# State-space stage of a hybrid trunk layer: later sums and products, and a decay table made by ScalarE

## The chip, the cores and the metric

The kernel runs on one core of a Trainium2 chip. The metric is the device time of one execution in microseconds (us), lower is better. The engines are TensorE (PE in the rows; PEld is its weight load), VectorE (DVE), ScalarE (ACT), GpSimd (POOL) and SyncE (SP, which issues most transfers). Each engine works through its own queue in order; the engines wait for one another by semaphores.

## What is computed

One layer of a decoder trunk over 512 positions of width 1024, all in fp32. The part that matters here is the state-space branch, a complex diagonal recurrence over 32 groups of 16 channels with 64 states each:

```python
mag = jnp.exp(lam_re * dt)                 # decay of a state in one step
a_re, a_im = mag * jnp.cos(ang), mag * jnp.sin(ang)
bu = jnp.einsum('bsgp,gnp->bsgn', ug, bb)  # real and imaginary part
h[t] = a * h[t - 1] + bu[t]                # complex, by an associative scan
y = Re(einsum('gpn,bsgn->bsgp', c, h)) + d_skip * u
y = gelu(y);  y = y * sigmoid(y @ w_glu)
```

Beside it the layer has a short convolution, windowed attention, three gated merges, a SwiGLU block and a per-layer embedding.

## The kernel before

TensorE multiplies large weights all the time. Every fp32 weight is split in two halves of lower precision: ACT makes `hi` (L245), DVE makes `lo = raw - hi` (L246), and three matmuls (L287 to L289) make one product; their results are the tiles called `z`. The state-space stage lies inside this work. It is written as a generator, `ssm_gen` (L1003), one for each of four tiles of 128 channels (tile 0 to tile 3). The function `slot` advances all running generators by one step, between two stretches of 24 large matmuls; a new tile starts every four slots, so two or three tiles are in flight at a time.

Inside a stretch the function `pump` is called after every three matmuls. Two tables hang on it. `peq` is a queue: a function put there runs at one of the next pumps. `later(d, f)` puts `f` into the program at the d-th pump from now. So both decide only the place of an instruction in the program; on the chip each engine then takes its own instructions in that order.

The steps of one tile, with their lines:
- E = t4(0)·pre + t4(1)·pim (L1026 DVE, L1027 POOL into `ewt`, L1028 the sum on DVE, called E-sum below). W is made in the same way a slot later (L1067 to L1069), with the same buffer `ewt`.
- `e_all` (L1059): TensorE transposes E (L1039) and makes K products (L1047), the E products below; ACT copies ET (L1040), ko and dbuf (L1053, L1054), and SP sends parts of dbuf (L1057).
- `v_two` (L1077): the v products (L1083) of inputs and ET; then `rotate(0)` and, two pumps later, `rotate(1)`.
- `rotate` (L1088), for each half: DVE makes the decay table `mt` (L1092): the fourth power of the decay, one number for each partition and group of columns, with the first column of each 128 set to zero. ACT copies two halves into `vsw` (L1095, L1096), DVE multiplies G (L1098, which reads PSUM), POOL multiplies vsw (L1099). Three pumps later `rot_in`: G-sub on DVE (L1102), the scan R (L1104), ACT's copies gsw (L1107, L1108), the products sv (L1111) and, on POOL, gsw (L1112), and four pumps later their sum (L1114).
- Two slots on, ACT copies dbuf into Dg (L1123); the next slot's first pump runs the y products (L1130 with Dg, L1132 with sv and W). ACT copies ys (L1137), SP sends it through memory and back.
- Three slots on: yc (L1155 DVE), qq = yc² (L1157 POOL), `poly` (L1163, L1164 DVE), a sigmoid (L1167 ACT), yu (L1168 DVE) and its split yh (L283 ACT), yl (L284 DVE). This falls into the slot in which E of the tile two further on is made.

Of the kernel before, what the change touches and what calls it, by code (L numbers as in the profile page):

```python
# [9 lines left out]
F32 = mybir.dt.float32  # L10
F32R = mybir.dt.float32r
I32 = mybir.dt.int32
AF = mybir.ActivationFunctionType
ALU = mybir.AluOpType
# [27 lines left out]
C_CM = 640  # L42
# [35 lines left out]
def hybrid_trunk_kernel(  # L78
# [7 lines left out]
    pe, act, dve, pool, sp = nc.tensor, nc.scalar, nc.vector, nc.gpsimd, nc.sync  # L86
# [5 lines left out]
    def open_pool(stack, name, bufs=1, **kw):  # L92
        return stack.enter_context(tc.tile_pool(name=name, bufs=bufs, **kw))
# [16 lines left out]
    def ps_t():  # L110
        return pst.tile([128, 512], F32, tag="t", name="t")
# [7 lines left out]
    def ccol(i, n=1):  # L119
        return cst[:, i:i + n]  # L120
# [161 lines left out]
    def split_ap(src, hi, lo):  # L282
        act.copy(out=hi, in_=src)  # L283
        later(2, lambda: dve.tensor_tensor(lo, src, hi.bitcast(F32), ALU.subtract))  # L284
# [6 lines left out]
    peq = deque()  # L291
    fine = []

    def later(d, fn):
        if state["delay"]:
            due.setdefault(state["pump"] + d, []).append(fn)
        else:
            fn()
# [90 lines left out]
    mag4 = const.tile([128, 32], F32, tag="mag4", name="mag4")  # L389
# [560 lines left out]
    for pair in range(2):  # L950
        cc, acc = [], []
        for i in range(2):
            ps = z_tile()
            c = cvp.tile([128, T], F32, tag="cc", name="cc", bufs=2)
# [3 lines left out]
        for i in range(2):  # L958
# [5 lines left out]
            a = cvp.tile([128, T], F32, tag="acc", name="acc", bufs=2)  # L964
# [28 lines left out]
    sp_ = open_pool(sst, "ssm", 2)  # L993
# [6 lines left out]
    SC = [128, 4, 128]  # L1000


    def ssm_gen(ct):  # L1003
        rows = slice(ct * 128, (ct + 1) * 128)
        g0, c0 = ct * 8, ct * TBW
# [11 lines left out]
        def t4(i):  # L1017
            return t3(i).unsqueeze(2).to_broadcast(SE)

        def p4(tab, m0):  # L1020
            return tab[:, g0:g0 + 8, m0:m0 + 4].unsqueeze(3).to_broadcast(SE)

        yield
        E = sp_.tile(SE, F32, tag="EW", name="E", bufs=3)
        tmp = sp_.tile(SE, F32, tag="ewt", name="ewt", bufs=1)
        dve.tensor_tensor(E, t4(0), p4(pre, 1), ALU.mult)  # L1026
        pool.tensor_tensor(tmp, t4(1), p4(pim, 1), ALU.mult)  # L1027
        dve.tensor_tensor(E, E, tmp, ALU.add)  # L1028
        yield
        ET = sp_.tile(SC, F32, tag="ET", name="ET", bufs=1)  # L1030
        kps = []
# [27 lines left out]
        def e_all():  # L1059
# [1 line left out]
            k_two(0)  # L1061
            k_two(2)

        peq.append(e_all)
        W = sp_.tile(SE, F32, tag="EW", name="W", bufs=3)
        tmp = sp_.tile(SE, F32, tag="ewt", name="ewt", bufs=1)
        dve.tensor_tensor(W, t4(2), p4(pre, 0), ALU.mult)  # L1067
        pool.tensor_tensor(tmp, t4(3), p4(pim, 0), ALU.mult)
        dve.tensor_tensor(W, W, tmp, ALU.add)  # L1069
        cs = sp_.tile([128, 2, 8, 128], F32, tag="cs", name="cs", bufs=1)  # L1070
        sp.dma_start(out=cs.rearrange("p a g c -> p a (g c)"),
                     in_=tb_d[:, c0 + 512:c0 + TBW].rearrange("p (a n) -> p a n", a=2))
        yield
        vps, svs = {}, {}


        def v_two(a):  # L1077
            if a == 0:
                for b in range(2):
                    vps[b] = ps_t().rearrange("p (a c) -> p a c", a=4)  # L1080
            for b in range(2):
                r = slice(64 * b, 64 * b + 64)
                pe.matmul(vps[b][:, a], ET[r, a], uu[r, a], start=True, stop=True)  # L1083
            if a == 3:
                rotate(0)
                later(2, lambda: rotate(1))

        def rotate(h):  # L1088
            v3 = vps[h]
            cosT, sinT = cs[:, 0, h::2], cs[:, 1, h::2]  # L1090
            mt = sp_.tile(SC, F32, tag="mt", name="mt")
            dve.tensor_tensor(mt, mag4[:, g0 + h:g0 + 8:2].unsqueeze(2).to_broadcast(SC),  # L1092
                              ccol(C_CM, 128).unsqueeze(1).to_broadcast(SC), ALU.mult)
            vsw = sp_.tile(SC, F32, tag="sa", name="vsw")
            act.copy(out=vsw[0:64], in_=v3[64:128])  # L1095
            act.copy(out=vsw[64:128], in_=v3[0:64])  # L1096
            G = sp_.tile(SC, F32, tag="sb", name="G", bufs=3)
            dve.tensor_tensor(G, v3, cosT, ALU.mult)  # L1098
            pool.tensor_tensor(vsw, vsw, sinT, ALU.mult)  # L1099

            def rot_in():
                dve.tensor_tensor(G, G, vsw, ALU.subtract)  # L1102
                R = sp_.tile(SC, F32, tag="sa", name="R")
                dve.tensor_tensor_scan(R.rearrange("p g c -> p (g c)"), mt.rearrange("p g c -> p (g c)"),  # L1104
                                       G.rearrange("p g c -> p (g c)"), 0.0, ALU.mult, ALU.add)
                gsw = sp_.tile(SC, F32, tag="sc", name="gsw")
                act.copy(out=gsw[0:64], in_=R[64:128])  # L1107
                act.copy(out=gsw[64:128], in_=R[0:64])  # L1108
                sv = sp_.tile(SC, F32, tag="sb", name="sv", bufs=3)
                dve.memset(sv[:, :, 0:1], 0.0)  # L1110
                dve.tensor_tensor(sv[:, :, 1:128], R[:, :, 0:127], cosT[:, :, 0:127], ALU.mult)  # L1111
                pool.tensor_tensor(gsw, gsw, sinT, ALU.mult)  # L1112
                svs[h] = sv
                later(4, lambda: dve.tensor_tensor(sv[:, :, 1:128], sv[:, :, 1:128], gsw[:, :, 0:127], ALU.add))  # L1114

            later(3, rot_in)

        peq.append(lambda: [v_two(a) for a in range(4)])
        yield
        yield  # L1120
        for b in range(2):
            r = slice(64 * b, 64 * b + 64)
            act.copy(out=Dg[r, :, r].rearrange("p a (i q) -> p a i q", q=16),  # L1123
                     in_=dbuf[r].rearrange("p i a q -> p a i q"))
# [29 lines left out]
        yc = sp_.tile(SC, F32, tag="ya", name="yc", bufs=1)  # L1154
        dve.scalar_tensor_tensor(yc, un[:, ::-1, :], vecs[:, ct:ct + 1], yr, ALU.mult, ALU.add)  # L1155
        qq = sp_.tile(SC, F32, tag="un", name="qq", bufs=1)
        pool.tensor_tensor(qq, yc, yc, ALU.mult)  # L1157
        yu = sp_.tile([128, T], F32, tag="yb", name="yu", bufs=1)
# [5 lines left out]
            dve.tensor_tensor(qq, qq, yc, ALU.mult)  # L1164

        later(2, poly)
        later(4, lambda: act.activation(out=qq, in_=qq, func=AF.Sigmoid, scale=1.5957691216057308))  # L1167
        later(5, lambda: dve.tensor_tensor(yu.rearrange("p (c i) -> p i c", i=4)[:, ::-1, :], yc, qq, ALU.mult))  # L1168
        later(7, lambda: split_ap(yu, ybox[0][0][:, ct], ybox[0][1][:, ct]))
        yield  # L1170

# [3 lines left out]
    def slot():  # L1175
        if slot_n[0] in SSM_SLOTS:
            bg.append(ssm_gen(SSM_SLOTS[slot_n[0]]))
        slot_n[0] += 1
        step()
# [318 lines left out]
```

## Time and profile before

| what | us |
|---|---|
| median of three runs (856.53 to 858.35) | 856.62 |
| the profiled execution | 857.07 |
| its span in the trace | 855.3 |
| TensorE busy | 837.7 (98%) |
| DVE busy | 559.9 (65%) |
| ACT busy | 383.8 (45%) |
| POOL busy | 123.6 (14%) |

TensorE is the busiest engine by far, but the end of a matmul is modelled in the trace, so its busy share hides short gaps; the distance of two starts shows them. The state-space stage lies between about 176 and 320 us.

### The profile page before, as it was taken

The numbers are of one execution on the slowest core, as the hardware profiler recorded it, in microseconds if no ns is written. First come the engines' busy times: TensorE is split into PE (matmuls) and PEld (weight loads), VectorE is DVE, ScalarE is ACT, GpSimd is POOL, SyncE is SP. The second block draws the span as 40 slices with busy tenths as digits, with TensorE's granted clock in tenths as the row PEclk, the third lists the DMA queues.
The fourth block names the chain that finished last, engine by engine and source line by source line (L and its number), as shares of the span: only waits on it lengthen the run. The fifth ranks groups of instructions, "written<-read, shape, count | busy, mean of one in ns | idle before, by whom it ended". The sixth has DMA issues, their size and how long they took to land.

```text
span 855.3 us, 10658 instructions
## 1 busy us (share of the span) xinstructions
PE 837.7 (98%) x4053; PEld 694.3 (81%) x4053; DVE 559.9 (65%) x850; ACT 383.8 (45%) x603; POOL 123.6 (14%) x118
## 2 busy tenths in 40 slices
PE   8999999999999999999999999999999999999996
PEld 6988778887877788888879888788888888888786
DVE  4889698848788864576775547554447444466864
ACT  6665657646444532443454333433333333334633
POOL 2031081724233311000002111000000000000001
PEclk9999999999999999999999999999999999999999
DMA  8759568553525359624858989982247432225112
GB/s 314 237 176 332 192 144 202 121 176 112 175 101 198 106 188 249 173 75 148 345 175 254 260 189 270 330 254 94 96 158 245 148 99 99 98 100 197 61 44 105
DMA packets 96034, 150.52 MB, mean 176 GB/s; under 512 B 6936, under 2 KB 66992, under 8 KB 93808
## 3 DMA queue, kind: packets, MB, share of 16 engines
q1 hardware_dynamic: 85200, 117.86, 40.6%
q0 software_dynamic: 10240, 31.46, 15.7%
q8 instruction: 32, 0.52, 0.2%
q10 hardware_dynamic: 544, 0.52, 0.2%
q14 instruction: 18, 0.15, 0.1%
HBM read 138.09 MB, written 43.00 MB: 212 GB/s over the span
## 4 chain that ended last, share of the span: by engine, by line
PE 68%; DVE 15%; ACT 5%; issue 4%; POOL 3%; DMA 3%; SPq 0%; POOLq 0%; DVEq 0%; ACTq 0%
PE z L287 16%; PE z L288 16%; PE z L289 16%; DVE lo L246 4%; PE z L1304 3%; PE z L1305 3%; PE z L1303 3%; DMA raw<-T 2%; PE z L1277 1%; PE z L1276 1%; PE z L1275 1%; DVE s_t L853 1%; PE z L683 1%; ACT s_t L867 1%; ACT hi L245 1%
## 5 line engine op out<-in xcount | busy, mean ns | idle before, releaser
L287 PE MATMUL z<-h,hi 128*128 128x512 f32 (+1 forms) x776 | 294.3, 379 | 0.0
L288 PE MATMUL z<-l,hi 128*128 128x512 f32 (+1 forms) x776 | 291.3, 375 | 0.8 <-DVE l L284 0.8
L289 PE MATMUL z<-h,lo 128*128 128x512 f32 (+1 forms) x776 | 291.0, 375 | 0.0
L246 DVE TENSOR_TENSOR lo<-raw,hi 128x1024 fp32r<-128x1024 f32 (+1 forms) x168 | 206.3, 1232 | 109.4 <-ACT hi L245 108.9
L245 ACT CAST hi<-raw 128x1024 fp32r<-128x1024 f32 (+1 forms) x168 | 171.8, 1031 | 135.9 <-PE z L1305 37.8
L289 PEld LDWEIGHTS z<-h,lo 128*128 128x128 f32 x776 | 146.9, 189 | 26.4
L287 PEld LDWEIGHTS z<-h,hi 128*128 128x128 f32 x776 | 147.0, 189 | 25.9 <-issue 1.2
L288 PEld LDWEIGHTS z<-l,hi 128*128 128x128 f32 x776 | 146.9, 189 | 26.0 <-DVE l L284 1.3
L1303 PE MATMUL z<-hi,fh 128*128 128x512 f32 x180 | 70.8, 393 | 0.0
L1304 PE MATMUL z<-lo,fh 128*128 128x512 f32 x180 | 70.2, 390 | 0.4 <-DVE lo L246 0.4
L1305 PE MATMUL z<-hi,fl 128*128 128x512 f32 x180 | 70.3, 391 | 0.0
L1333 POOL TENSOR_TENSOR rs<-ms,nhalf 128x1 f32<-128x1 f32 x8 | 6.2, 771 | 345.3 <-DVE ms L1332 345.3
L1390 DVE TENSOR_TENSOR g<-z,g 128x512 f32<-128x512 f32 x22 | 15.2, 691 | 62.0 <-PE z L289 62.0
L287 PE MATMUL z<-yh,hi 128*128 128x512 f32 x112 | 44.0, 393 | 0.0
L288 PE MATMUL z<-yl,hi 128*128 128x512 f32 x112 | 43.7, 390 | 0.2 <-DVE yl L284 0.2
L289 PE MATMUL z<-yh,lo 128*128 128x512 f32 x112 | 43.6, 390 | 0.0
L1304 PEld LDWEIGHTS z<-lo,fh 128*128 128x128 f32 x180 | 33.8, 188 | 7.6 <-DVE lo L246 0.8
L1305 PEld LDWEIGHTS z<-hi,fl 128*128 128x128 f32 x180 | 33.8, 188 | 7.4 <-DVE fl L284 0.5
L1303 PEld LDWEIGHTS z<-hi,fh 128*128 128x128 f32 x180 | 33.8, 188 | 6.7
L1382 ACT ACTIVATE g<-z 128x512 f32<-128x512 f32 x22 | 13.2, 598 | 49.8 <-PE z L289 49.8
L283 ACT CAST fh<-g 128x512 fp32r<-128x512 f32 (+1 forms) x22 | 11.2, 511 | 53.0 <-DVE g L1390 53.0
L1310 DVE TENSOR_TENSOR xr<-z,xr 128x512 f32<-128x512 f32 x36 | 24.3, 683 | 8.4 <-PE z L1305 7.4
(274 smaller groups left out, 1084.9 us busy)
## 6 DMA issues: line engine op xcount, KB each, us to landing
raw<-in_w_in_dram SPq DMA_DIRECT2D x23, 1024.0 KB, 5.3
raw<-in_w_ffn_in_dram SPq DMA_DIRECT2D x22, 1024.0 KB, 5.1
raw<-T SPq DMA_DIRECT2D x12, 1024.0 KB, 4.9
T<-in_w_ffn_out_dram POOLq DMA_DIRECT2D x12, 1024.0 KB, 12.2
T<-in_w_out_dram POOLq DMA_DIRECT2D x6, 1024.0 KB, 9.6
raw<-in_w_branch_dram SPq DMA_DIRECT2D x12, 512.0 KB, 3.9
raw<-in_w_ffn_out_dram SPq DMA_DIRECT2D x6, 1024.0 KB, 4.9
T<-in_w_ffn_out_dram POOLq DMA_DIRECT2D x6, 768.0 KB, 8.1
```

The source lines that it names most:

```text
L245: act.copy(out=hi, in_=src)
L246: todo = [lambda: dve.tensor_tensor(lo, src, hi.bitcast(F32), ALU.subtract)]
L283: act.copy(out=hi, in_=src)
L287: pe.matmul(ps, wh, ah, start=first, stop=False)
L288: pe.matmul(ps, wh, al, start=False, stop=False)
L289: pe.matmul(ps, wl, ah, start=False, stop=last)
L1303: pe.matmul(ps, fh[:, f, kk, ts], hi[:, k], start=st, stop=False, skip_group_check=True)
L1304: pe.matmul(ps, fh[:, f, kk, ts], lo[:, k], start=False, stop=False, skip_group_check=True)
L1305: pe.matmul(ps, fl[:, f, kk, ts], hi[:, k], start=False, stop=last, skip_group_check=True)
L1310: dve.tensor_tensor(dst, ps if sign > 0 else dst, dst if sign > 0 else ps, ALU.add if sign > 0 else ALU.subtract)
L1382: act.activation(out=g[:, i], in_=ps, func=AF.Silu)
L1390: dve.tensor_tensor(g[:, i], ps, g[:, i], ALU.mult)
```

## The change

Five edits in `ssm_gen`. The sums E-sum and W's sum are put two pumps later. `e_all` goes from `peq` to the third pump. The v products go from `peq` (first pump) to the third. The table `mt` is no longer one DVE multiplication for each half; ACT makes it, in four activations of 128 columns (the constant row times one column of `mag4`), at pumps 1 and 2 of the slot of the v products. The sigmoid and yu go from pumps 4 and 5 to 5 and 6.

```diff
-        dve.tensor_tensor(E, E, tmp, ALU.add)
+        later(2, lambda E=E, tmp=tmp: dve.tensor_tensor(E, E, tmp, ALU.add))
...
-        peq.append(e_all)
+        later(3, e_all)
...
-        dve.tensor_tensor(W, W, tmp, ALU.add)
+        later(2, lambda W=W, tmp=tmp: dve.tensor_tensor(W, W, tmp, ALU.add))
...
-        vps, svs = {}, {}
+        vps, svs, mts = {}, {}, {}
+
+        def decay(h):
+            mts[h] = mt = sp_.tile(SC, F32, tag="mt", name="mt")
+            for a in range(4):
+                act.activation(out=mt[:, a], in_=ccol(C_CM, 128), func=AF.Copy, scale=mag4[:, g0 + 2 * a + h:g0 + 2 * a + h + 1])
+
+        for h in range(2):
+            later(1 + h, lambda h=h: decay(h))
...
-            mt = sp_.tile(SC, F32, tag="mt", name="mt")
-            dve.tensor_tensor(mt, mag4[:, g0 + h:g0 + 8:2].unsqueeze(2).to_broadcast(SC),
-                              ccol(C_CM, 128).unsqueeze(1).to_broadcast(SC), ALU.mult)
+            mt = mts[h]
...
-        peq.append(lambda: [v_two(a) for a in range(4)])
+        later(3, lambda: [v_two(a) for a in range(4)])
...
-        later(4, lambda: act.activation(out=qq, in_=qq, func=AF.Sigmoid, scale=1.5957691216057308))
-        later(5, lambda: dve.tensor_tensor(yu.rearrange("p (c i) -> p i c", i=4)[:, ::-1, :], yc, qq, ALU.mult))
+        later(5, lambda: act.activation(out=qq, in_=qq, func=AF.Sigmoid, scale=1.5957691216057308))
+        later(6, lambda: dve.tensor_tensor(yu.rearrange("p (c i) -> p i c", i=4)[:, ::-1, :], yc, qq, ALU.mult))
```

The order that follows, engine by engine (a name with a number is one buffer; new lines stand up to 8 numbers higher from L1069 on). ACT in tile 0, before, from the weight half `hi` of the v products' slot on:

```order
L245 CAST hi_2081<-raw_1989 128x1024
L1095 COPY vsw_2102<-t_2090 64x512
L1096 COPY vsw_2102<-t_2090 64x512
L1095 COPY vsw_2116<-t_2091 64x512
L1096 COPY vsw_2116<-t_2091 64x512
L1107 COPY gsw_2129<-R_2127 64x512
L1108 COPY gsw_2129<-R_2127 64x512
L1198 COPY merged_1925<-z_2086 128x512
```

and after:

```order
L245 CAST hi_2081<-raw_1988 128x1024
L1079 ACTIVATE mt_2090<-cst_84,mag4_111 128x128 x4
L1079 ACTIVATE mt_2098<-cst_84,mag4_111 128x128 x4
L1101 COPY vsw_2116<-t_2106 64x512
L1102 COPY vsw_2116<-t_2106 64x512
L1204 COPY merged_1925<-z_2086 128x512
L1101 COPY vsw_2131<-t_2107 64x512
L1102 COPY vsw_2131<-t_2107 64x512
L1113 COPY gsw_2143<-R_2141 64x512
```

Eight activations now stand between hi and the first vsw copy, and a copy of a large product between the two pairs of vsw.

DVE in tile 0, from the first mt on, before (R is the scan):

```order
L1092 TENSOR_TENSOR mt_2100<-mag4_111,cst_84 128x512
L1098 TENSOR_TENSOR G_2105<-t_2090,cs_2026 128x512
L1092 TENSOR_TENSOR mt_2114<-mag4_111,cst_84 128x512
L1098 TENSOR_TENSOR G_2119<-t_2091,cs_2026 128x512
L246 TENSOR_TENSOR lo_2082<-raw_1989,hi_2081 128x1024
L1102 TENSOR_TENSOR G_2105<-G_2105,vsw_2102 128x512
L1104 SCALAR_TENSOR_TENSOR R_2127<-mt_2100,G_2105 128x512
```

and after:

```order
L1104 TENSOR_TENSOR G_2119<-t_2106,cs_2025 128x512
L246 TENSOR_TENSOR lo_2082<-raw_1988,hi_2081 128x1024
L1104 TENSOR_TENSOR G_2134<-t_2107,cs_2025 128x512
L1108 TENSOR_TENSOR G_2119<-G_2119,vsw_2116 128x512
L1110 SCALAR_TENSOR_TENSOR R_2141<-mt_2090,G_2119 128x512
```

Both mt are gone, and lo moved from behind the second G to between the two.

DVE where tile 0 ends and tile 2 begins, from yc on, before (qq twice is `poly`):

```order
L1155 SCALAR_TENSOR_TENSOR yc_2459<-un_2285,vecs_113,yr_2332 128x512
L1026 TENSOR_TENSOR E_2468<-tb_2414,pre_109 128x512
L1028 TENSOR_TENSOR E_2468<-E_2468,ewt_2469 128x512
L1163 TENSOR_SCALAR qq_2461<-qq_2461 128x512
L1164 TENSOR_TENSOR qq_2461<-qq_2461,yc_2459 128x512
L246 TENSOR_TENSOR lo_2474<-raw_2337,hi_2473 128x1024
L1168 TENSOR_TENSOR yu_2463<-yc_2459,qq_2461 128x4x128
```

and after:

```order
L1161 SCALAR_TENSOR_TENSOR yc_2471<-un_2290,vecs_113,yr_2338 128x512
L1026 TENSOR_TENSOR E_2480<-tb_2425,pre_109 128x512
L1169 TENSOR_SCALAR qq_2473<-qq_2473 128x512
L1170 TENSOR_TENSOR qq_2473<-qq_2473,yc_2471 128x512
L1028 TENSOR_TENSOR E_2480<-E_2480,ewt_2481 128x512
L246 TENSOR_TENSOR lo_2485<-raw_2343,hi_2484 128x1024
L1174 TENSOR_TENSOR yu_2475<-yc_2471,qq_2473 128x4x128
```

E-sum moved from ahead of poly's two steps to behind them. On TensorE the E products stand two pumps later in tile 0 and one pump later in tiles 1 to 3, the v products two pumps later in all four; the y products stay where they were.

## Rows read from the trace of the kernel before

**Rows 1.** Busy time by window: the stretch, busy us (instructions) by engine, clock, DMA.

```profile
176.00:346.00 170.00, 167.87 (x841) 135.44 (x841) 121.39 (x146) 75.72 (x123) 44.45 (x37) 1.00 0.55 167
```

**Rows 2.** TensorE's waits, 176 to 346 us: waiter, releaser, total us, times, longest.

```profile
PE t L1083 <- ACT ET L1040: 1.1, 2, 0.6
PE t L1039 <- DVE E L1028: 0.7, 1, 0.7
```

**Rows 3.** Timeline of TensorE at tile 0's y products: start, duration, line, output, inputs.

```profile
209.66 0.39 PE L288 MATMUL z<-l,hi 128*128 128x512 f32 x1
209.88 0.39 PE L289 MATMUL z<-h,lo 128*128 128x512 f32 x1
210.24 0.46 PE L1130 MATMUL t<-uu,Dg 128*128 128x128 f32 x2
```

**Rows 4.** ACT, scaled activations of 128 columns: one group, two in the timeline.

```profile
L882 ACT ACTIVATE s_t<-s_t,dn 128x128 f32<-128x128 f32 x4 | 1.4, 396 | 1.8 <-DVE dn L878 1.8
...
97.22 0.69 ACT L882 ACTIVATE s_t<-s_t,dn 128x128 f32<-128x128 f32 x2
```

**Rows 5.** Timeline of ACT, tile 0: hi, the first vsw copy, the Dg copies.

```profile
192.47 1.05 ACT L245 CAST hi<-raw 128x1024 fp32r<-128x1024 f32 x1
193.75 0.58 ACT L1095 COPY vsw<-t 64x512 f32<-64x512 f32 x1 [0.23 <-PE t L1083]
...
209.32 0.82 ACT L1123 COPY Dg<-dbuf 64x256 f32<-64x256 f32 x2
```

**Rows 6.** Timeline of DVE, tile 0: first G, second mt, lo, G-sub.

```profile
194.96 0.69 DVE L1098 TENSOR_TENSOR G<-t,cs 128x512 f32<-128x512 f32 x1 [3.41 <-ACT vsw L1096]
195.57 1.28 DVE L1092 TENSOR_TENSOR mt<-mag,cst 128x512 f32<-128x512 f32 x1
...
197.37 1.71 DVE L246 TENSOR_TENSOR lo<-raw,hi 128x1024 fp32r<-128x1024 f32 x1
199.00 0.68 DVE L1102 TENSOR_TENSOR G<-G,vsw 128x512 f32<-128x512 f32 x1
```

**Rows 7.** Timeline of POOL, tile 0: both products of vsw.

```profile
195.01 2.99 POOL L1099 TENSOR_TENSOR vsw<-vsw,cs 128x512 f32<-128x512 f32 x2 [11.69 <-ACT vsw L1096]
```

**Rows 8.** Timeline of DVE and of POOL, tile 1, where W is made.

```profile
211.34 1.22 DVE L246 TENSOR_TENSOR lo<-raw,hi 128x1024 fp32r<-128x1024 f32 x1
212.48 1.55 DVE L1067 TENSOR_TENSOR W<-tb,pre 128x512 f32<-128x512 f32 x1
...
211.51 1.97 POOL L1068 TENSOR_TENSOR ewt<-tb,pim 128x512 f32<-128x512 f32 x1 [3.15 <-DVE E L1028]
```

**Rows 9.** Timeline of DVE, from yc of tile 0 to yu.

```profile
237.89 0.74 DVE L1155 SCALAR_TENSOR_TENSOR yc<-un,vecs,yr 128x512 f32<-128x512 f32 x1
...
241.18 0.69 DVE L1028 TENSOR_TENSOR E<-E,ewt 128x512 f32<-128x512 f32 x1 [1.95 <-POOL ewt L1027]
241.78 0.42 DVE L1163 TENSOR_SCALAR qq<-qq 128x512 f32<-128x512 f32 x1
...
243.59 1.21 DVE L246 TENSOR_TENSOR lo<-raw,hi 128x1024 fp32r<-128x1024 f32 x1
244.73 1.07 DVE L1168 TENSOR_TENSOR yu<-yc,qq 128x512 f32<-128x512 f32 x1
```

**Rows 10.** Timeline of POOL in the same slot.

```profile
238.71 1.42 POOL L1157 TENSOR_TENSOR qq<-yc 128x512 f32<-128x512 f32 x1 [3.02 <-DVE yc L1155]
240.09 1.05 POOL L1027 TENSOR_TENSOR ewt<-tb,pim 128x512 f32<-128x512 f32 x1
```

**Rows 11.** Timeline of ACT, from yh of tile 0 to vsw of tile 2.

```profile
245.83 0.62 ACT L283 CAST yh<-yu 128x512 fp32r<-128x512 f32 x1 [1.49 <-DVE yu L1168]
...
251.03 0.58 ACT L1095 COPY vsw<-t 64x512 f32<-64x512 f32 x1
```

**Rows 12.** Timelines of ACT and TensorE, tile 3: Dg and the first y product.

```profile
294.53 0.82 ACT L1123 COPY Dg<-dbuf 64x256 f32<-64x256 f32 x2
...
295.99 0.38 PE L1130 MATMUL t<-uu,Dg 128*128 128x128 f32 x2
```

## The prediction

> **What bounds the kernel now.** I read the table by window of the state-space stage first, then TensorE's waits in it, then the timelines of ACT, DVE and POOL round the tiles. TensorE is busy for nearly the whole stage, at a granted clock of 1.00, the 2.4 GHz level [rows 1], so only its few waits can give time, and any new wait costs time one for one. It waits 1.1 us in two places for the copy ET and 0.7 us for the sum E [rows 2]; these stand at the start of the v products and of the E products of tiles 2 and 3. The total to be won is therefore about 1.8 us, 0.2% of the kernel. Against it stand TensorE's y products, which need the block Dg from ACT: for tile 0 they start at 210.24 [rows 3], 0.10 us after the second Dg copy ends (209.32 + 0.82 = 210.14 [rows 5]). So that place has no slack at all: what makes Dg later there makes TensorE later.
>
> The chain behind Dg runs, in every tile, from the v products over ACT's vsw copies, DVE's G and G-sub (L1102), the two scans, ACT's gsw copies, to Dg. I call the start of the first vsw copy V.
>
> **Tile 0: eight activations in front of vsw.** ACT takes its work in order, and in the new order the eight mt activations stand between hi and vsw. Two activations of the same shape, with a column as scale, took 0.69 us, so the second started 0.30 us after the first (0.69 less the mean of one, 0.396) [rows 4]; eight are 2.4 us. hi starts at 192.47 and takes 1.05 us, of which about 0.1 overlaps the next [rows 5], so the eight run from 193.43 to 195.85. Today V is 193.75: V moves by +2.1 us. The v products themselves are two pumps later, 2 x 3 matmuls at a distance of 0.22 to 0.23 us [rows 3], 1.4 us. Today vsw starts right behind them; at 193.75 + 1.4 = 195.15 they are still covered by ACT's 195.85.
>
> DVE gives something back. Today G starts at V+1.21, then the second mt takes 1.28 us (a sum of the same shape takes 0.69 [rows 9]), lo takes 1.71 us (1.21 alone [rows 9]), and G-sub starts at 199.00 = V+5.25 [rows 6]. POOL has its two products from 195.01 to 198.00 [rows 7]. The lengths fit if a DVE operation with both inputs in SBUF and a POOL operation keep each other out: POOL's first product, then mt, then POOL's second, then lo from 197.9 to 199.1. G, which reads PSUM, is not lengthened. In the new order (G, lo, G, G-sub) that gives: POOL's first product V+1.26 to V+2.32 (1.06 us), lo V+2.32 to V+3.5, POOL's second V+3.5 to V+4.56, the second G beside it, G-sub at V+4.56. So 0.7 us comes back, although an mt of 1.28 us left: lo and POOL have taken its place. G-sub is 2.1 - 0.7 = 1.4 us later, and so is everything behind it to Dg, whose order is unchanged: **+1.4 us** of TensorE wait at tile 0's y products, with all later z products queued behind it.
>
> **Tile 1** is released by TensorE's v products again, which are those 1.4 us late, and repeats the same order on ACT and DVE: its chain is 1.4 + 1.4 = 2.8 us late.
>
> **Tiles 2 and 3: a loop that sets the time.** From here DVE and ACT feed themselves. G-sub of a tile leads with unchanged steps to yc of the tile before; yc leads to E, poly, yu, yh, ACT's queue, V of the next tile and its G-sub. Counting from yc = t (237.89 today [rows 9]): POOL's qq ends at t+2.24 and its ewt runs from t+2.20 to t+3.25 [rows 10]. Today E-sum comes at t+3.29, then poly, lo at t+5.70, yu, and yh on ACT at 245.83 = t+7.94 [rows 9, 11]. Put behind poly, E-sum comes later: poly's first step t+2.3 to t+2.75, its second kept out by ewt until t+3.25 and done at t+3.9, E-sum t+3.9 to t+4.55 (today it ends at t+3.98). That is 0.57 us later, and the E products stand 0.7 us (one pump) later in TensorE's queue, so this wait by itself neither goes nor grows. lo then runs t+4.5 to t+5.7 and yu would start at t+5.65, yh at t+6.75: 1.2 us earlier than today. But POOL's second ewt is let go by E-sum at t+4.6, while lo runs. Exactly this stands in the trace of tile 1: lo at 211.34 for 1.22 us, ewt asked for at 211.51 and taking 1.97 us, the DVE operation after lo taking 1.55 us, where one of that shape takes 0.69 [rows 8, 9]. If yu suffers that, it is done 0.9 to 1.1 us later, yh is at t+7.75, only 0.2 us earlier.
>
> *By a page:* the Trainium skill, "SBUF — State Buffer", Who interferes with whom, states that the pair of ports is locked for a whole instruction by whoever starts first, and that DVE's tensor_scalar can take it too. The trace agrees on tensor_tensor by the lengths above; for the tensor_scalar, 0.42 us [rows 9], no row shows it asked for while POOL is at work. If poly's first step waits too, E-sum ends at t+4.9, each loop grows by 0.35 us and the time would be 0.7 us above the one below.
>
> From yh to V ACT's queue has no gap to spare: 245.83 to 251.03 [rows 11], 5.20 us; the eight activations lengthen it by 2.4 us to 7.6. The v products don't set V there. V to G-sub gives back 0.7 us as before. One loop: (-1.2 to -0.2) + 2.4 - 0.7 = **+0.5 to +1.5 us**. I take +1.0: the precedent of rows 8 speaks for the upper end, but yu, a longer strided operation (1.07 us), has no row beside POOL. Two loops, into tile 2 and into tile 3: +1.0 to +3.0, taken as +2.0.
>
> **Edits at nothing.** W's sum put later is needed only at the y products, four slots on; E's sum for tiles 0 and 1 has no poly in front. The mt products themselves are off DVE's path except the one counted. The sigmoid and yu one or two places of the count later keep their order on ACT and DVE, which were waiting for data there. SP and POOL issue the same transfers in the same order; the ones behind ko and ys shift with their sources and land long before use.
>
> **The sum.** Tile 3's chain is 2.8 + 2.0 = 4.8 us late. Today its Dg ends at 294.53 + 0.82 = 295.35 and TensorE uses it at 295.99 [rows 12]; with 0.10 for the hand-over the slack is 0.54. TensorE leaves the stage 4.8 - 0.54 = 4.26, about **4.2 us**, later (3.3 to 5.3 by the ends of the loop). The waits for ET go, but they are inside this sum: the chain's end decides, not the waits before it. Behind the stage TensorE is the bound again and nothing gives the time back. Eight activations at 0.25 or 0.35 us would move each of the four tiles by 0.4 us, so I widen the ends to 2.5 and 5.7. The profiled execution took 857.07 us (span 855.3 us and 1.8 around it); with 4.2 it is 861.3. The median of the three runs is 0.45 us lower, so **860.8 us**, from 859.1 to 862.3.
>
> **The rivals.**
> *POOL does not keep DVE out where I put it*, or DVE always gets in first. Then G-sub comes at V+3.6 (G, lo 1.2, G, each start 0.6 to 1.2 after the last), 1.65 us earlier; tile 0 costs 0.4 us, a loop -1.2 + 2.4 - 1.65 = about -0.5, and TensorE keeps the 1.1 us of ET and half of E's 0.7: 0.4 - 1.1 - 0.4 = -1.1, **855.5 us**. Against it: mt 1.28 and lo 1.71 [rows 6], W 1.55 [rows 8].
> *ACT has the time and DVE does not*: DVE is busy 121 of 170 us, ACT 76 [rows 1]; if vsw is not really held by the activations, all waits of rows 2 go: 1.8 to 2.0 us, **854.7 us**, faster. Against it: the order, and ACT's gapless rows 5 and 11. The Trainium skill, "Perfetto Trace Analysis", Optimizing Scalar/DVE Operations, is for this one: with DVE saturated, moving work to ScalarE may pay. The trace agrees on the load, not on the queue.
> *The edits cancel or miss*: tile 0's +1.4 and the ET waits' -1.1 are all that is felt: **856.9 us**. It needs tiles 1 to 3 to have over 1.4 us of slack before Dg; tile 3 has 0.54.
>
> **How the numbers follow.** My forecast, slower by 2.5 to 5.7 us: 0.64. The first rival 0.15, the second 0.13, the third 0.08. 0.2% of this time, 1.7 us, is about what a measurement can tell from no change. Faster by more: the second rival and little else, 0.14. Within it: the first and the third, 0.22. Slower: 0.64. The range must reach past the first rival and part of the second: 855.0 to 862.3 leaves about 0.08 below and 0.08 above.
>
> **What would show it.** Right: TensorE starts tile 0's y products about 1.4 us after it could (near 211.6), later ones of tiles 1 to 3 waiting for ACT's Dg; eight activations of 0.3 us spacing between hi and vsw; no wait for ET left; lo between the two G lengthened by POOL to about 1.7 us; yu lengthened to about 2 us where ewt is waiting. Wrong: y products that start without a wait, or vsw following the v products directly.

## The result, and the profile after

| | before | after |
|---|---|---|
| median of six runs, us | 857.21 (856.53 to 858.35) | 862.98 (861.64 to 866.12) |
| profiled execution (span), us | 857.07 (855.3) | 862.86 (861.1) |
| mean granted TensorE clock of it | 0.996 | 0.991 |

The ratio is 1.0073, 95% interval 1.0057 to 1.0089: slower by 5.8 us by the medians, where 4.2 us were forecast and the range ended at 862.3. The direction was right, the size was not.

The waits of TensorE in the stage, 176 to 346 us, in the profile of after (waiter, releaser, us in total, times, longest):

```profile
PE t L1039 <- DVE E L1028: 3.1, 2, 1.6
PE t L1136 <- issue: 1.5, 1, 1.5
PE t L1136 <- ACT Dg L1129: 0.8, 1, 0.8
```

Against [rows 2]: the waits for ET are gone, as forecast, the wait for Dg at tile 0's y products is there (1.5, forecast 1.4; the profile names "issue", but the Dg copies below end at 208.79 + 0.82 = 209.61, 0.09 us before these products start), and those for E have grown from 0.7 to 3.1, which was not forecast. ACT, DVE and TensorE of tile 0 in after (start, duration, then line, output, inputs):

```profile
190.41 1.05 ACT L245 CAST hi<-raw 128x1024 fp32r<-128x1024 f32 x1
191.35 2.44 ACT L1079 ACTIVATE mt<-cst,mag 128x128 f32<-128x128 f32 x8
193.81 0.58 ACT L1101 COPY vsw<-t 64x512 f32<-64x512 f32 x1
...
195.62 1.82 DVE L246 TENSOR_TENSOR lo<-raw,hi 128x1024 fp32r<-128x1024 f32 x1
197.96 1.18 DVE L1108 TENSOR_TENSOR G<-G,vsw 128x512 f32<-128x512 f32 x1
...
208.79 0.82 ACT L1129 COPY Dg<-dbuf 64x256 f32<-64x256 f32 x2
...
207.82 0.39 PE L289 MATMUL z<-h,lo 128*128 128x512 f32 x1
209.70 0.46 PE L1136 MATMUL t<-uu,Dg 128*128 128x128 f32 x2 [1.50 <-issue]
214.28 0.80 PE L287 MATMUL z<-h,hi 128*128 128x512 f32 x1
```

The eight activations stand between hi and vsw and take 2.44 us; lo between the two G takes 1.82 where POOL works beside it (1.71 before, [rows 6]). But the last row has something that no row of before had in this stage: a z product of 0.80 us where [rows 3] have 0.39. The table by window of after says why (stretch, then busy us and instructions of PE, PEld, DVE, ACT, POOL, granted clock, DMA):

```profile
210.00:214.00 4.00, 4.00 (x24) 2.39 (x22) 3.90 (x5) 2.10 (x3) 1.97 (x1) 0.59 0.88 296
214.00:218.00 4.00, 4.00 (x18) 3.06 (x14) 2.43 (x4) 0.66 (x2) 0.00 (x0) 0.55 0.72 271
218.00:222.00 4.00, 4.00 (x22) 3.44 (x22) 0.00 (x0) 1.17 (x4) 0.00 (x0) 1.00 0.32 77
248.00:252.00 4.00, 4.00 (x14) 3.28 (x14) 3.93 (x6) 2.08 (x4) 0.92 (x1) 0.57 0.00 0
```

Behind the wait of 1.5 us at 209.70, and again behind one of 1.56 us for E at 247.02, the granted clock is at its 1.2 GHz level for some microseconds. So two questions stood after the result: is the loss the waits, the clock behind them, or both; and is it the activations on ACT or the later places?

**How the steps are compared.** TensorE reaches tile 0's y products between 207.8 and 212.8 us in the traces of this study, though nearly all of them run the same instructions up to the stage; a single execution's time is uncertain by that much. So I count from the last z product ahead of tile 0's y products and give the distance between the starts that the chain passes: y0 (first product with Dg of tile 0), V1, V2, V3 (first vsw copy of tiles 1 to 3), y3. Before: y0 is in [rows 3], V2 in [rows 11], y3 in [rows 12]; V1 and V3 are these rows of ACT in before:

```profile
221.64 0.58 ACT L1095 COPY vsw<-t 64x512 f32<-64x512 f32 x1 [0.29 <-PE t L1083]
...
279.45 1.05 ACT L245 CAST hi<-raw 128x1024 fp32r<-128x1024 f32 x1 [0.63 <-PE t L1083]
280.40 0.58 ACT L1095 COPY vsw<-t 64x512 f32<-64x512 f32 x1
```

All kernels by these steps, in us (one profiled execution each, starts taken from the timelines):

| kernel | to y0 | y0 to V1 | V1 to V2 | V2 to V3 | V3 to y3 | in all |
|---|---|---|---|---|---|---|
| before | 0.36 | 11.39 | 29.40 | 29.36 | 15.60 | 86.11 |
| after, first profile | 1.88 | 16.43 | 31.34 | 30.52 | 14.39 | 94.56 |
| after, second profile (a2_after) | 1.88 | 13.51 | 31.33 | 30.49 | 14.70 | 91.91 |
| places only (e1_places) | 2.33 | 12.73 | 30.18 | 30.13 | 15.63 | 91.00 |
| activations only (e2_act) | 2.05 | 18.11 | 31.31 | 30.53 | 14.58 | 96.58 |
| after, mt in the first slot (e3_early) | 1.12 | 12.77 | 29.03 | 28.94 | 15.00 | 86.86 |
| before, mt in the first slot (e4_act_early) | 0.23 | 11.30 | 28.97 | 28.80 | 15.71 | 85.01 |
| after, E-sum ahead of poly (f1_esum_first) | 1.89 | 13.44 | 31.38 | 31.15 | 14.41 | 92.27 |
| before, a wait of 2.9 us (d10_dose) | 3.28 | 15.99 | 29.41 | 29.30 | 15.67 | 93.65 |
| the same, the wait filled (h2_fill_dose) | 3.31 | 11.38 | 29.40 | 29.33 | 15.63 | 89.05 |
| after, all long waits filled (h4_fill_all) | 1.94 | 13.44 | 31.33 | 30.52 | 14.40 | 91.63 |
| after, y0 wait filled (h1_fill_y0) | 1.94 | 13.45 | 31.32 | 30.49 | 14.73 | 91.93 |
| after, E waits filled (h3_fill_e) | 1.88 | 13.46 | 31.33 | 31.94 | 15.00 | 93.61 |
| before, a wait of 1.4 us (d5_dose) | 1.82 | 11.38 | 29.41 | 29.17 | 15.81 | 87.59 |
| e4 with E and ewt earlier, v later (f2_early_e) | 0.44 | 12.06 | 28.99 | 28.93 | 14.86 | 85.29 |
| version that beats both (f3_late_yh) | 0.23 | 11.30 | 27.68 | 28.84 | 15.00 | 83.05 |

The first profile of after is 8.45 us longer by this count and only 5.8 in its time, because it had reached the stage 2.06 us earlier (207.82 against 209.88: the trace of before has 3.4 us at the lower clock at 36 us, this one has not), and the stretch behind the stage was 0.6 us shorter.

### The profile page after: what moved, and what is told of

It reads as the page before. It is cut to its first block, busy times and chain, and to the rows that moved or that the text cites. A ratio compares the mean times of both kernels' runs of the same rounds, so it can differ in the third digit from the quotient of the medians.

```text
span 861.1 us, 10680 instructions
## 1 busy us (share of the span) xinstructions
PE 841.1 (98%) x4053; PEld 695.7 (81%) x4053; DVE 556.1 (65%) x842; ACT 392.7 (46%) x635; POOL 126.1 (15%) x118
## 4 chain that ended last, share of the span: by engine, by line
PE 71%; DVE 14%; ACT 5%; issue 5%; POOL 3%; DMA 1%; POOLq 0%; SPq 0%; DVEq 0%; ACTq 0%
PE z L287 16%; PE z L288 16%; PE z L289 16%; PE z L1311 4%; PE z L1309 4%; PE z L1310 4%; DVE lo L246 3%; PE z L1283 1%; PE z L1282 1%; PE z L1281 1%; PE z L683 1%; ACT hi L245 1%; DVE xn L1346 1%; ACT s_t L867 1%; DVE xr L1316 1%
```

## The experiments

**The places alone.** The kernel after with the table made by DVE again.

```diff
-            mt = mts[h]
+            mt = sp_.tile(SC, F32, tag="mt", name="mt")
+            dve.tensor_tensor(mt, mag4[...], ccol(C_CM, 128)..., ALU.mult)
```

> The later places alone: the kernel after with the decay table mt made by DVE again, as before. Theory 1 (the eight activations ahead of vsw on ACT make Dg late, and the granted clock falls behind the longest of the waits): the v products stand two pumps later, so vsw starts 1.4 us later at tile 0 and the y products there wait about 1.4 us, but the loops of tiles 2 and 3 lose the 2.4 us of activations; 858 to 861 us, with at most one fall of the clock, at tile 0. Theory 2 (the places alone are the cause, E-sum behind poly above all): about 863 us as the kernel after, E products waiting 1.7 us for E. Theory 3 (the falls of the clock have nothing to do with waits): waits sum to about 3 us less than after, falls anywhere.

Measured: 864.44 us, ratio 1.0089 (1.0061 to 1.0118). My theory gave 858 to 861: it fell here, and theory 2 was near. DVE of this kernel at tile 0:

```profile
195.99 0.69 DVE L1097 TENSOR_TENSOR G<-t,cs 128x512 f32<-128x512 f32 x1 [4.86 <-ACT vsw L1095]
196.59 1.81 DVE L246 TENSOR_TENSOR lo<-raw,hi 128x1024 fp32r<-128x1024 f32 x1
198.33 1.78 DVE L1091 TENSOR_TENSOR mt<-mag,cst 128x512 f32<-128x512 f32 x1
200.03 0.68 DVE L1097 TENSOR_TENSOR G<-t,cs 128x512 f32<-128x512 f32 x1
200.63 0.68 DVE L1101 TENSOR_TENSOR G<-G,vsw 128x512 f32<-128x512 f32 x1
```

Two pumps later, vsw comes 1.4 us later (as forecast for the v products), and lo and the second mt now meet both products of POOL: each is lengthened (1.81 and 1.78; in [rows 6] 1.71 and 1.28). G-sub starts 5.85 us behind V, not 5.25. In all, the places alone make the stage 4.9 us longer.

**The activations alone.** The kernel before with mt by ACT at the start of the slot of the v products.

```diff
+        for h in range(2):
+            decay(h)
...
-            dve.tensor_tensor(mt, mag4[...], ccol(C_CM, 128)..., ALU.mult)
+            mt = mts[h]
```

> The activations alone: the kernel before with mt made by eight activations on ACT at the start of the slot of the v products, all places as before. Theory 1: vsw starts 2.1 to 2.4 us later in each tile, 0.7 us comes back on DVE, y products of tile 0 wait about 1.7 us, the clock falls to the 1.2 GHz level behind that; 861 to 863.5 us. Theory 2: about 857 us, since no place is moved. Theory 3: waits of theory 1, but the clock stays or falls elsewhere; 859 to 861 us.

Measured: 865.04 us, ratio 1.0091 (1.0062 to 1.0121). As theory 1 has it, but 1.5 us beyond the end of its range; the clock stood at the lower level for 10.2 us behind the wait of 1.7 us at y0. So each half of the change costs about as much as the whole, or more. They overlap: the same 2.4 us of ACT hide the v products' delay, and taking mt from DVE removes what the later places made longer.

**The activations where ACT has time.** The kernel after, with `decay(0)` and `decay(1)` in the first of the tile's slots that works, where E is made.

```diff
         yield
+        for h in range(2):
+            decay(h)
         E = sp_.tile(SE, F32, tag="EW", name="E", bufs=3)
...
-        for h in range(2):
-            later(1 + h, lambda h=h: decay(h))
```

> The kernel after with the eight activations moved to the first slot of the tile, where E is made and ACT has idle time, so that nothing of them stands between hi and vsw. Theory 1: vsw follows the v products (1.4 us later than before at tile 0, 0.7 given back on DVE), y products of tile 0 wait about 0.7 us, no wait for ET, no fall of the clock; 856 to 858.5 us. Theory 2: 862 to 863 us, since the places are those of after. Theory 3: the waits of theory 1 with falls of the clock by chance.

Measured: 859.13 us, ratio 1.0022 (1.0006 to 1.0037), 0.6 us above the end of the range. The waits of this kernel in the stage:

```profile
PE t L1048 <- DVE E L1037: 2.4, 2, 1.3
PE t L1136 <- issue: 0.7, 1, 0.7
```

The wait for Dg is the forecast 0.7, and both loops are 2.3 and 1.6 us shorter than in after. Not forecast were the waits for E, 2.4 us. So where the activations stand is worth about 4 us, and what stays is the later place of the v products and of E.

**The same with the places of before.** `decay` as in the last diff, all else as before.

```diff
-            dve.tensor_tensor(mt, mag4[...], ccol(C_CM, 128)..., ALU.mult)
+            mt = mts[h]
```

> The kernel before, all its places kept, with mt made by ACT in the first slot of the tile, where ACT has idle time. Theory 1 (what stands ahead of vsw on ACT, and the place of the v products, set Dg): with neither moved against Dg and both mt gone from DVE, G-sub comes 0.7 us earlier, the y products of tile 0 don't wait, the waits for ET (0.64 twice) stay, those for E shrink or stay; 855.5 to 857.7 us, no fall of the clock behind a wait. A rival (a table made by ACT and read by DVE's scan costs time wherever it is made): over 859 us.

Measured: 857.61 us, ratio 0.9990 (0.9978 to 1.0003): as expected, no difference that the runs can show, though by the steps the stage is 1.1 us shorter. A table made by ACT costs nothing that the runs can show; the place in its queue did.

**One wait, and the clock.** The kernel before with n idle activations ahead of tile 0's Dg, n = 5 (1.5 us) and n = 10 (3.0 us).

```diff
+        if ct == 0:
+            pad = sp_.tile(SC, F32, tag="pad", name="pad", bufs=1)
+            for a in range(n):
+                act.activation(out=pad[:, a % 4], in_=ccol(C_CM, 128), func=AF.Copy, scale=mag4[:, a:a + 1])
```

> The kernel before with five idle activations of 128 columns (into a tile that nobody reads, 0.3 us each, 1.5 us together) just ahead of the Dg copies of tile 0. One wait of about 1.5 us at tile 0's y products is put in, and nothing else. Theory 1: the granted clock falls to the 1.2 GHz level behind the wait, as in the kernel after, and the time grows by 1.5 for the wait and 2 to 3.4 for the clock: 860.5 to 862. Theory 3: no fall there, 1.5 alone: 858.7.

Measured for n = 5: 859.26 us, ratio 1.0021 (1.0007 to 1.0035). The wait is there (1.4 us in the trace), and no fall behind it in the profiled execution. Of the twelve executions ten show a mean clock of 0.996 to 0.998 and 857.88 to 859.97 us, two show 0.990 and 863.18 and 863.39 us. No trace was taken of these two. As before shows no mean clock under 0.993 in 23 executions, I take them for falls behind the wait: at this length a fall comes in some executions and not in others, here 2 in 12, and costs about 4 us where it comes.

> As the run with five idle activations ahead of tile 0's Dg, now ten, 3.0 us. Without a fall of the clock: 857.7 + 3.0 = 860.7 less what was slack in the first dose, about 860.4. If the chance of a fall grows with the length of the wait, more than the 2 of 12 executions of the first dose show a mean clock of 0.992 or less and some 4.4 us on top: median up to 865. If falls behind a wait are chance at any length, again about 2 of 12.

Measured for n = 10: 864.45 us, ratio 1.0071 (1.0052 to 1.0089), mean clock 0.994 or less in all six executions (before: 0.993 to 0.998): the wait of 2.9 us brought a fall in the profiled execution and, as far as mean clocks can tell, in the others. In the trace (TensorE at tile 0's y products, then the granted clock by window):

```profile
211.11 0.39 PE L289 MATMUL z<-h,lo 128*128 128x512 f32 x1
214.39 0.46 PE L1134 MATMUL t<-uu,Dg 128*128 128x128 f32 x2 [2.89 <-POOL ewt L1068]
...
216.24 0.80 PE L1134 MATMUL t<-uu,Dg 128*128 128x128 f32 x2
```

```profile
218.00:222.00 4.00, 4.00 (x18) 3.06 (x17) 2.95 (x5) 1.10 (x2) 0.00 (x0) 0.50 0.14 40
```

The releaser named, POOL's ewt, had long been done; what ended the wait is the Dg copies, which only the idle activations made late. From y0 to V1 it takes 15.99 us in place of 11.39: the fall cost 4.6 us.

**The same wait, filled.** Three products of 512 columns on TensorE in that wait, into the PSUM tile that the y products then overwrite.

```diff
+            for _ in range(3):
+                pe.matmul(yps, uu[:, 0], uu.rearrange("p a n -> p (a n)"), start=True, stop=True)
```

> The kernel before with ten idle activations ahead of tile 0's Dg, and three products of 512 columns on TensorE in the wait that these make (some 2.6 of 2.9 us). Theory 1: the clock stays, 857.7 + 2.9 = 860.6, against 864.45 with the wait left empty. Rival: 864.5, as with the wait empty.

Measured: 861.71 us, ratio 1.0045 (1.0029 to 1.0062); 1.1 us above the expectation, but 2.7 below the empty wait (2.2 by the ratios, each to before on its own chip; their intervals overlap a little, so the rows below count for more). TensorE in this kernel, and the window behind:

```profile
211.80 0.39 PE L289 MATMUL z<-h,lo 128*128 128x512 f32 x1
212.03 2.73 PE L1134 MATMUL t<-uu 128*128 128x512 f32 x6
215.11 0.46 PE L1140 MATMUL t<-uu,Dg 128*128 128x128 f32 x2 [0.35 <-ACT Dg L1127]
```

```profile
216.00:220.00 4.00, 4.00 (x31) 2.95 (x31) 3.83 (x6) 2.39 (x5) 0.00 (x0) 1.00 0.77 312
```

The y products start as late as with the empty wait (3.31 against 3.28 behind the last z product), but the clock stays at 1.00 and y0 to V1 is 11.38. All six executions have a mean clock of 0.995 or more; with the wait empty none had. That TensorE stood still is what brought the clock down.

**Is E-sum behind poly the culprit?** The kernel after, E-sum at once again.

```diff
-        later(2, lambda E=E, tmp=tmp: dve.tensor_tensor(E, E, tmp, ALU.add))
+        dve.tensor_tensor(E, E, tmp, ALU.add)
```

> The kernel after with E-sum alone put back ahead of poly; all else of the change stays. Theory 1 (poly's first step waits for POOL's ewt, and E-sum behind it makes E 0.9 us later): the E products of tiles 2 and 3 wait 0.3 to 0.9 us in place of 1.74, y products of tile 0 still 1.66; 860.5 to 861.8 us. Rival (E is late because the loop from yc to V is longer, wherever E-sum stands): E products still wait 1.5 us or more, 863 us.

Measured: 864.43 us, ratio 1.0079 (1.0054 to 1.0105): no gain. The waits of this kernel:

```profile
PE t L1136 <- ACT Dg L1129: 4.6, 2, 2.4
PE t L1136 <- issue: 1.5, 1, 1.5
PE t L1039 <- DVE E L1028: 1.4, 2, 0.7
```

The E waits fell from 3.1 to 1.4 us, as theory 1 said, and the wait for Dg at tiles 2 and 3 rose from 0.8 to 4.6. So neither theory was right: neither loop is shorter than in after (31.38 and 31.15, against 31.34 and 30.52), and TensorE arrives earlier only to wait at the next place. An E wait here is a sign of the loop, not a cause.

**Filling the waits of after.** Two products of 512 columns ahead of tile 0's y products (h1); two ahead of the E products of tiles 2 and 3 (h3); all these and also two ahead of tile 2's y products and one ahead of tile 3's (h4), beside the kernel after on the same chip (a2). For the E products:

```diff
         def e_tr():
             pt = ps_t()
+            for _ in range({2: 2, 3: 2}.get(ct, 0)):
+                pe.matmul(pt, ident, tb, start=True, stop=True)
```

> The kernel after, with two products of 512 columns (some 0.85 us each, into the PSUM tile that the y products then overwrite) put on TensorE just ahead of tile 0's y products, so that it is at work while it would wait for Dg. Theory 1 (the clock falls because TensorE stands still for 1.5 us there, and that costs 3.0 us between tile 0's y products and tile 1's vsw on top of the wait): no fall behind tile 0's y products, about 3 us less than after, 859.5 to 860.5. Rival (the fall is no consequence of the wait, or its cost is covered by later waits): 862.5 to 863.5.

Measured: 864.04 us, ratio 1.0073 (1.0053 to 1.0092). No fall behind tile 0's y products, and y0 to V1 is 13.45 in place of 16.43; but the time is not lower. TensorE waited 1.5 us at tile 2's y products in its place, and the clock fell there.

> The kernel after, with two products of 512 columns put on TensorE just ahead of the E products of tile 2 and of tile 3, in their waits of 1.74 us. Theory 1 (from tile 1's vsw on the time is set by the loop over DVE and ACT, G-sub, yc, yh, vsw, in which TensorE has no part; the E waits and the second fall of the clock are covered by it): no fall there and no gain, 862.5 to 863.5. Rival (each wait and each fall costs its time): 1.5 to 2 us less than after, 861 to 861.5.

Measured: 865.29 us, ratio 1.0088 (1.0071 to 1.0106). No gain, as theory 1 said, but a loss of a kind that it had not: in the profiled execution the clock fell behind a wait at tile 2's y products, the filling ahead of tile 3's E products then ran at the lower clock, and V2 to V3 took 31.94 us. E was done at 277.01; its products had to stand behind the filling, and ACT's `hi` ahead of the activations waited for TensorE:

```profile
277.62 2.78 PE L1039 MATMUL t<-tb,cst 128*128 128x512 f32 x4
280.24 0.60 PE L1041 MATMUL t<-cst,E 128*128 128x128 f32 x4
...
284.96 1.05 ACT L245 CAST hi<-raw 128x1024 fp32r<-128x1024 f32 x1 [1.30 <-PE z L288]
```

So TensorE's lost time is free in the loop only as far as ACT does not come to wait for it.

> The kernel after once more, on the same chip as the next run. 862.5 to 864; in some executions one or two falls of the clock in the stage, in others none.

Measured: 863.63 us, ratio 1.0074 (1.0054 to 1.0094). The six executions have mean clocks from 0.989 to 0.996.

> The kernel after with products of 512 columns on TensorE in all of its longer waits: two ahead of the y products of tile 0, two ahead of the E products of tile 2 and of tile 3, two ahead of the y products of tile 2, one ahead of those of tile 3. Theory 1 (chain and falls both count): no fall in the stage; the chain alone is left, 5.3 to 5.8 us later than before at the end of the stage by the steps measured without a fall; 862 to 863, and 1 to 2 us less than the kernel after beside it. Rival A (the falls are nearly all of the loss): 859 to 860. Rival B (the falls cost nothing, later waits take them in): the same time as the kernel after beside it.

Measured: 863.68 us, ratio 1.0064 (1.0048 to 1.0081): the same median as the kernel after beside it (rival B), with no fall in any part of the stage and no wait left but one of 0.2 us:

```profile
176.00:346.00 170.00, 169.63 (x834) 133.31 (x833) 116.03 (x136) 82.95 (x153) 45.96 (x36) 1.00 0.52 159
```

TensorE is busy throughout here, and nothing is gained that the runs can show. The means of the two differ by 0.7 us, and six executions of each do not tell that from nothing, nor from the lower end of theory 1. So one loop, in two traces, has to decide. The second profile of after has a fall of 6.8 us behind a wait at tile 2's y products (row by row: the wait and the wide third product; then the window):

```profile
272.35 0.49 PE L1136 MATMUL t<-uu,Dg 128*128 128x128 f32 x2 [1.58 <-ACT Dg L1129]
...
273.92 0.75 PE L1136 MATMUL t<-uu,Dg 128*128 128x128 f32 x2
```

```profile
274.00:281.00 7.00, 7.00 (x28) 5.21 (x28) 6.03 (x7) 0.63 (x1) 4.41 (x3) 0.51 0.15 60
```

and yet its V2 to V3 is 30.49 us, against 30.52 in h4 without a fall. From V1 on the chain runs over ACT and DVE; what TensorE loses there, it would have waited.

**A version that beats both.** If the loop from yc over yh to vsw holds E and ET, two ways are open: make E earlier, or take yh out of ET's way. For f2, in the first-slot version (e4):

```diff
+        later(6, e_mul)
         yield
...
-        dve.tensor_tensor(E, t4(0), p4(pre, 1), ALU.mult)
-        pool.tensor_tensor(tmp, t4(1), p4(pim, 1), ALU.mult)
...
-        peq.append(lambda: [v_two(a) for a in range(4)])
+        later(2, lambda: [v_two(a) for a in range(4)])
```

where `e_mul` holds the two removed products.

> A version built from what the runs so far show: mt by ACT in the first slot, the products of E and ewt one slot earlier (ahead of yc and of POOL's qq), the v products one pump later than before. Theory 1: no wait for E (0.24 and 0.90 before) and none for ET (0.64 twice and 0.18 inside), y products of tile 0 no later, since G-sub gains the 0.7 us that the v products lose; 2.0 to 2.8 us less than before: 854.9 to 855.7. Rival (the waits only move, to Dg of tiles 1 to 3): 857 to 858 us.

Measured: 856.65 us, ratio 0.9991 (0.9978 to 1.0004). The E waits went, those for ET stayed (1.0 us in two places): no difference to be shown, and above the expected range.

For f3 the first-slot version (e4) was changed in three places, for tiles 0 to 2:

```diff
-        later(4, lambda: act.activation(out=qq, in_=qq, func=AF.Sigmoid, ...))
-        later(5, lambda: dve.tensor_tensor(yu..., yc, qq, ALU.mult))
-        later(7, lambda: split_ap(yu, ...))
+        later(4 if ct == 3 else 6, ...)
+        later(5 if ct == 3 else 8, ...)
+        later(7 if ct == 3 else 11, ...)
```

> The version with mt made by ACT in the first slot and the places of before, and in it, for tiles 0 to 2, the sigmoid 2 pumps, yu 3 and the split yh 4 pumps later, so that on ACT yh stands behind ET, ko and dbuf and these no longer queue behind a copy that waits for yu. Theory 1 (the loop from yc over yh to vsw is what makes ET and E late): the waits for ET (0.64 and 0.18 in each of tiles 2 and 3) and for E go; 1.5 to 2.5 us less than before: 855.5 to 856.5. Rival (ET is held by hi and ys ahead of it in ACT's queue): 857.6, no gain on the same version without it.

Measured: 855.38 us, ratio 0.9967 (0.9955 to 0.9979): faster than before by 2.8 us by the ratio (1.9 by the medians), and than after, on other chips, by some 8. ACT of this version between tiles 0 and 2, and TensorE's only wait in the stage:

```profile
246.51 0.59 ACT L1049 COPY ET<-t 128x512 f32<-128x512 f32 x1
...
247.46 0.24 ACT L1063 COPY dbuf<-ko 128x64 f32<-128x64 f32 x1
247.61 0.61 ACT L283 CAST yh<-yu 128x512 fp32r<-128x512 f32 x1
...
249.80 0.58 ACT L1102 COPY vsw<-t 64x512 f32<-64x512 f32 x1
```

```profile
PE z L288 <- DVE yl L284: 0.2, 1, 0.2
```

yh stands behind ET now, and no longer delays it by its wait for yu. The E and ET waits of [rows 2] are gone, and none has come in their place.

## Why the prediction was wrong in size

**Right.** The mechanism and its places: eight activations of 0.30 us ahead of vsw; y0 late by 1.52 (forecast 1.4); tile 1 released by TensorE's v products and late again, y0 to V1 by 2.12 us in the execution without a fall there (forecast: G-sub 2.8 late, V 0.7 more, less y0's 1.4, so 2.1); no wait for ET; lo and yu lengthened beside POOL (1.82, 1.95); the loop over ACT and DVE that sets the time from tile 1 on. Behind V3 0.90 came back (forecast 1.24: 0.7 at G-sub and 0.54 of slack). Of the later y products one waited in each profile (tile 3's 0.84 us, tile 2's 1.58 us), not those of all three tiles; the E waits ahead of them took that time. The first rival needed POOL to leave DVE alone (lo took 1.82), the second vsw to be free of the activations, the third slack before Dg in tiles 1 to 3; none of this was so.

**The term that was mis-sized: the loop.** Taken +1.0 for each, +2.0 in all; measured 31.33 - 29.40 = +1.93 and 30.49 - 29.36 = +1.13, in all 3.06. With the others: 1.52 + 2.12 + 3.06 - 0.90 = 5.80 us, which is what the stage lost in the second profile of after and, within its interval, what the timed runs show. The sum of the forecast differs from it by 1.5 us, of which the loops are 1.06; the first loop lies outside its own bounds of +0.5 to +1.5, the second inside. Another 0.6 us of the distance from 860.8 to 862.98 is no step of the kernel: the median of before was 856.62 in three executions and is 857.21 in six. The steps of the first loop in that profile, DVE's and ACT's:

```profile
226.60 0.58 ACT L1101 COPY vsw<-t 64x512 f32<-64x512 f32 x1
230.75 1.17 DVE L1108 TENSOR_TENSOR G<-G,vsw 128x512 f32<-128x512 f32 x1
238.96 1.26 DVE L1217 TENSOR_TENSOR merged<-merged,sg 128x512 f32<-128x512 f32 x1 [0.67 <-ACT sg L1192]
242.47 0.74 DVE L1161 SCALAR_TENSOR_TENSOR yc<-un,vecs,yr 128x512 f32<-128x512 f32 x1
244.75 1.27 DVE L1169 TENSOR_SCALAR qq<-qq 128x512 f32<-128x512 f32 x1 [0.93 <-POOL qq L1163]
246.67 0.68 DVE L1028 TENSOR_TENSOR E<-E,ewt 128x512 f32<-128x512 f32 x1
248.40 1.95 DVE L1174 TENSOR_TENSOR yu<-yc,qq 128x512 f32<-128x512 f32 x1
250.38 0.62 ACT L283 CAST yh<-yu 128x512 fp32r<-128x512 f32 x1 [2.97 <-DVE yu L1174]
257.93 0.58 ACT L1101 COPY vsw<-t 64x512 f32<-64x512 f32 x1
```

- yh follows yc by 7.91 us; before it was 7.94 ([rows 9, 11]). I had taken 0.7 off, the middle between 1.2 and 0.2. The 1.2 us that E-sum's move should free were eaten twice: yu took 1.95 (which I had seen coming, and priced at about 1 us), and poly's first step took 1.27 in place of 0.42 ([rows 9]), because it too waits for POOL's ewt, which runs from 244.68 to 245.74 there. That is the rule of the Trainium skill, "SBUF — State Buffer", Who interferes with whom, which I had set beside the sum and not into it: by it each loop was to be 0.35 us longer. The trace agrees with it: E-sum ends 4.88 us behind yc, where that sentence of the prediction had 4.9.
- G-sub starts 4.15 us behind V and not 4.56, but takes 1.17 itself, with POOL's second product beside it; and one of the two merged sums behind it now waits 0.67 for ACT's sigmoid. So the steps from G-sub to yc, which the prediction took as unchanged, went from 11.01 to 11.72 us. Together V to yc gave back 0.37 us in the first loop and 0.43 in the second, not 0.7.
- yh to V grew by 2.35 us in the first loop (forecast 2.4) and by 1.62 in the second. There ACT had 0.63 us of idle time in before (the row of hi at 279.45 above): "no gap to spare" was read from tile 2 and held only there.

**"Any new wait costs time one for one"** failed on both sides. At y0, where TensorE releases the next step, a wait can cost more than its length: the fall behind it cost 3.0 us in the first profile of after (16.43 against 13.44 in h4) and 4.6 with the 2.9 us wait. From V1 on the waits of after cost nothing that shows: h4 has none of them and loops of the same length. That the E wait "neither goes nor grows" was wrong (3.1 us in the first profile), and it did not matter.

**What stays open.** In the first profile of after a fall at y0 is paid for; in the second there is none there, and the stage is 2.65 us shorter, with nearly the same time, since one reached the stage 3.4 us before the other. The median of six such executions does not tell what the falls add to it. The traces bear out the 5.8 us of the chain without them. h2 stands 4.4 us above before (its interval is 2.5 to 5.3) and its stage is only 2.94 us longer; in its profiled execution 1.92 us more lie ahead of that count (211.80 against 209.88), where the idle activations have no part.

## What to carry to other kernels

Before work is moved to an engine that is idle on average, look at what stands next in that engine's queue at the place where it will be issued; here the same eight activations cost about 4 us ahead of vsw and nothing that shows two slots earlier. Where a chain over two other engines sets the time, a wait of the busy engine is only its sign: follow one loop from start to start, price each of its steps by rows, and test a wait by filling it before you try to remove it. And where the queue of an engine holds a copy that waits for late data, what stands behind it (here ET behind yh) is where time is to be won.

## What the runs showed of the hardware that was not expected

- Waits of TensorE far shorter than I had thought of can bring the granted clock down, and not each time: of 18 waits of 1.4 to 2.4 us in the stage, in the profiled executions of after and of the variants, 7 were followed by a stretch at the 1.2 GHz level, of 3.4 to 10.2 us; the wait of 2.9 us was followed by one, and the mean clocks of its six executions suggest the same of all. Behind waits of 1.3 us and less in the stage there was none. Work that is thrown away, done in the wait, kept the clock there.
- The same instructions ahead of the stage took between 207.8 and 212.8 us to get there; part of it is one stretch of 3.4 us at the lower clock near 36 us, which 11 of the 16 traces have. Differences below some 2 us were to be seen only by steps inside one trace.
- DVE's tensor_scalar with one input was kept out while POOL's tensor_tensor ran: 1.27 us in place of 0.42.
- The length of the wait is not all of it. The stretch near 36 us has no wait that the profile shows in the 10 us ahead of it; what stands there is small products (16 of 32 columns in 1.93 us in before). And a wait of 1.5 to 1.6 us near 122 us, ahead of the stage, is in all 16 traces, and no fall follows it in any. What else decides is open. In before that wait is this row of TensorE:

```profile
122.81 0.39 PE L848 MATMUL t<-KH,Q 128*128 128x256 f32 x1 [1.55 <-DVE Pl L284]
```
